# A decoder layer's mixer: the block inverses' transfers move from SyncE's to GpSimd's queue, small GpSimd operations move to VectorE and ScalarE, r, k and v get their own buffer ring, and the ordering model's DMA trips are doubled

## Chip, cores, metric

One core of one Trainium2 chip. The metric is the device time of one launch in microseconds; lower is better.

## What is computed

One step of one hybrid layer for 320 tokens (a prompt of 256 and eight samples of 8), in float32. Cut to what matters here:

```
p = x @ w_in                               # 2048 -> 5408 columns
y_lru  = conv4 -> gated linear recurrence (8 blocks of 128 channels) * gelu(gate)
y_rwkv = RWKV-7: r, k, v with token shift, per token and head (16 heads of 64)
         S = S*w - (S kk) (kk a)^T + v k^T ;  o = S r ; group norm ; gate
x = LN(a*x + [y_lru, y_rwkv] @ w_out)
x = LN(a*x + cross-attention(x, mem))      # mem_k = mem @ wk, mem_v = mem @ wv
x = LN(a*x + relu(x @ w1)^2 @ w2)          # 2048 -> 8192 -> 2048
```

All states (S of prompt and samples, shift rows, convolution rows, recurrence) are outputs too.

## The kernel before

Every weight streams from memory once, in pieces of 128 x 1024 float32 on SyncE's queue (`Stream.load`, L320), three pieces ahead. ScalarE rounds a piece to float32r (`wh<-wraw`), VectorE makes the rest (`wl<-wraw,wh`), and TensorE does three matmuls for each 128 x 128 tile: wh times the high part of the activations, wh times the low part, wl times the high part. These "large matmuls" fill TensorE nearly all the time.

The mixer is the first stage. `linear("w_in", ...)` makes 43 column tiles: three of codes, then for each of eight pairs of heads r, k, v, x, g (48 large matmuls per tile). `linear("wk", ...)` follows with 16 tiles. Beside them run small tasks, written as generators: `rwkv(p)` (L673) for the pair p, `invert(p)` (L885), `sample(p)` (L967) and `lru_task(i)` (L1022).

For the pair p, `rwkv` makes Gram matrices on TensorE (`ps<-AR,BK`), VectorE masks them into the tile GM, and `invert` inverts the triangular blocks of GM: GM goes to memory (bm, two transfers of 64 x 5 x 64, L892), comes back as 40 blocks of 16 x 16 (Mp, L898), GpSimd inverts them in 30 small operations (`tt<-Mp,Xp`, `Xp<-Xp,tt`), Xp goes to memory (bx, L912) and comes back in columns (Xn, two transfers, L917). Then VectorE transposes Xn into XT, and TensorE joins the blocks in four small steps (`ps<-Xn,GM 32x16` is the first, `ps<-XT,Z 32x32` the last). With XT, `rwkv` walks through four chunks, one after the other: R (`ps<-S,AR`, `ps<-UV,GM`), `ps<-R,XT`, copy to UV, `ps<-UV,BT`, new state S. Then come the group norm (`ps<-t,KM`, the spread `ps<-qg,K`) and the gate. The norm's square root and the copies are on ScalarE and VectorE.

All engines work in order, and the order is set when the kernel is built: `Sched` (from L120) keeps a model clock of TensorE and of V, A and G (VectorE, ScalarE, GpSimd). `account` (L136) adds a modelled cost for every operation; `Sched.dma` (L179) puts a task 2.5 us later in the model for a trip to memory; between large matmuls `tick` (L210) puts in the small steps that the model takes to be ready. `drain` (L245) runs tasks without large matmuls between them, until a named task is over: when v of pair i is there, `rwkv(i-3)` must be over (L1099); at x of i, the recurrence i-1 (L1110). The model has no cost for what really happens on the chip; its only effect is the order.

In the order stand on GpSimd's queue, besides the inverses: memset of a column of the scan's tile P (L710), two copies of decays into PT (L777, L778), the memset of `a0` before the recurrence's scan (L1064), a memset and a copy for the convolution (L1108, L1109), and the stores of the states Sp and Ss (L849, L1012), later the stores of mk. On SyncE's queue stand the weights and the inverses' six transfers, and the loads of lora, S0, mem.

Temporaries (`tmp`, L565) come from one ring of 16 buffers; z of r, k, v, which live through most of `rwkv`, come from it as well.

Of the kernel before, what the change touches and what calls it, by code (L numbers as in the profile page):

```python
# [9 lines left out]
F32 = mybir.dt.float32  # L10
# [8 lines left out]
NTOK = 320  # L19
# [85 lines left out]

NTMP = 16
NPB = 3
# [12 lines left out]
class Sched:  # L120
# [15 lines left out]
    def account(self, e, op, a, k):  # L136
# [19 lines left out]
        if e == "V":  # L156
            c = (0.06 + 6.5e-3 * n if op == "reciprocal" else 0.12 + 2.3e-3 * n if op == "tensor_tensor_scan" else
                 0.15 + 1.05e-3 * n)
        elif e == "A":
            c = 0.2 + 0.85e-3 * n  # L160
            f = TABLE.get(a[2]) if op == "activation" else None
            if f is not None:
                if self.table not in f:
                    self.table = f[0]
                    c += 1.3
        else:
            c = 0.15 + 2.1e-3 * n
        t = self.clock if self.cur is None else max(self.clock, self.cur.t)
# [9 lines left out]

    def dma(self, t=2.5):  # L179
        if self.cur is not None:  # L180
            self.cur.t = max(self.clock, self.cur.t) + t
# [163 lines left out]
def body(ctx, tc, I, O):  # L345
# [194 lines left out]
    with ExitStack() as mx_ctx:  # L540
        tp = mx_ctx.enter_context(tc.tile_pool(name="tmp", bufs=NTMP))
        pp = mx_ctx.enter_context(tc.tile_pool(name="pair", bufs=NPB))
        p2 = mx_ctx.enter_context(tc.tile_pool(name="pair2", bufs=2))
# [68 lines left out]
        def blocks(t, h):  # L612

            return bass.AP(tensor=t.tensor, offset=t.offset + 4 * h * MS, ap=[[64, 64], [8 * MS, 5], [1, 64]])
# [4 lines left out]
        def seqs(ap):  # L619
            return ap[:, NP:NTOK].rearrange("p (b t) -> p b t", t=8)  # L620
# [20 lines left out]
        def c5(ap):  # L641
            return ap.rearrange("p (c t) -> p c t", t=64)
# [30 lines left out]
        def rwkv(p, zr, zk, zv):  # L673
# [35 lines left out]
            P = tmp(1 + NTOK)  # L709
            G.memset(P[:, 0:1], 1.0)  # L710
            V.tensor_tensor_scan(P[:, 1:], d0, d1, 0.0, op0=mult, op1=add)
# [64 lines left out]
            PT = pp.tile([128, 12], F32, name="PT")  # L776
            G.tensor_copy(PT[:, 0:4], c5(P1)[:, 0:4, 63])  # L777
            G.tensor_copy(PT[:, 4:12], seqs(P1)[:, :, 7])  # L778
            while sch.alive(("rwkv", p - 2)):
# [68 lines left out]
            yield  # L848
            nc.gpsimd.dma_start(O["Sp"][p], S)  # L849
            o = tmp()  # L850
# [34 lines left out]
        def invert(p, GM, res):  # L885
# [5 lines left out]
            for h in range(2):  # L891
                nc.sync.dma_start(blocks(bm[b], h), GM[HS[1 - h], h, :, 0, :])  # L892
            sch.dma()
# [3 lines left out]
            yield  # L897
            nc.sync.dma_start(Mp, diag(bm[b]))  # L898
            Mp = Mp.rearrange("p c r -> p r c")
# [4 lines left out]
            for j in range(15):  # L904
# [5 lines left out]
                if j % 5 == 4:  # L910
                    yield
            nc.sync.dma_start(diag(bx[b]), Xp)  # L912
            sch.dma()
            yield
            Xn = p1.tile([128, 5, 64], F32, name="Xn")
            for h in range(2):
                nc.sync.dma_start(Xn[HS[1 - h]], blocks(bx[b], h))  # L917
            sch.dma()
# [48 lines left out]
        def sample(p, S0, AR, XT, GM, B4, UV, PT, res):  # L967
# [43 lines left out]
            tt(S0, S0, PT[:, 4:12].unsqueeze(2).to_broadcast([128, 8, 64]), mult)  # L1011
            nc.gpsimd.dma_start(O["Ss"][p], S0)  # L1012

# [8 lines left out]
        def lru_task(i, ue):  # L1022
# [40 lines left out]
            tt(r0, r0, t8, add)  # L1063
            G.memset(a0, 0.0)  # L1064
            yield
# [19 lines left out]
        def on_win(m, ps):  # L1085
# [8 lines left out]
            elif kind in "rkv":  # L1094
                t = tmp()
                shifted({"r": 0, "k": 8, "v": 16}[kind] + i, ps, t)
# [6 lines left out]
            elif kind == "x":  # L1103
# [3 lines left out]
                A.copy(us[:, :, 3:11], ps[:, NP:NTOK].rearrange("p (b t) -> p b t", t=8))  # L1107
                G.memset(ue[:, 0:3], 0.0)  # L1108
                G.tensor_copy(us[:, :, 0:3], vec("cv", 24 * i, 24).rearrange("p (b t) -> p b t", t=3))  # L1109
                sch.drain(("lru", i - 1))  # L1110
# [620 lines left out]
```

## Time and profile before

| | us |
|---|---|
| median of 3 runs (lowest, highest) | 2060.48 (2059.3, 2062.53) |
| the profiled execution | 2060.96 |
| its span | 2059.2 |
| TensorE busy (96% of the span) | 1986.5 |
| VectorE, ScalarE, GpSimd busy | 1049.3, 890.4, 407.6 |
| mean granted TensorE clock, of full speed | 0.981 |

The page gives the busy time of each engine and then forty slices of the span; the mixer with its w_in and wk is slices 1 to 12 (0 to about 600 us). Times in the trace are from the start of the span. "Idle before <- X" is the idle time of an engine ahead of an instruction and what ended it. An operation's line is nearly always L284, the helper that records it, so instructions are told apart by their tiles: out<-in.

### The profile page before, as it was taken

To read this page: it belongs to the slowest core of one execution; us is meant where nothing else is said; L and a number is where in the kernel's file an instruction comes from. 1 tells how busy PE (TensorE), PEld (TensorE's weight loads), DVE (VectorE), ACT (ScalarE), POOL (GpSimd) and SP (SyncE) were. 2 spreads that over 40 slices of the span, in tenths; PEclk is the share of its full clock that TensorE was granted. 3 is DMA by queue.
4 is the path that set the end of the run, shared out by engine and by line. 5 is a ranking of instruction groups with operands and counts; after the bars stand their busy time and mean duration, and the time that the engine had idled before them with its cause. 6 is when DMAs were issued, how large, how long until landed. Compare 5 with 4: busy or idle time off the path is not lost.

```text
span 2059.2 us, 38107 instructions
## 1 busy us (share of the span) xinstructions
PE 1986.5 (96%) x15750; PEld 1889.1 (92%) x15750; DVE 1049.3 (51%) x1608; ACT 890.4 (43%) x1459; POOL 407.6 (20%) x677
## 2 busy tenths in 40 slices
PE   7989989998999999999999999999999999999996
PEld 7987878887898999988899999999999999999996
DVE  5566566666555445544466544443444444443444
ACT  5555455554535434643434633334323333233333
POOL 0121222220411244422143500001000000001133
PEclk9999999998999999999999999999999999999998
DMA  6443343333557764688744444444444444444442
GB/s 236 149 120 93 94 116 117 111 118 126 168 170 238 251 224 156 208 322 298 268 138 139 140 149 152 151 147 153 148 150 153 144 154 151 147 153 149 149 147 89
DMA packets 120846, 333.80 MB, mean 162 GB/s; under 512 B 33072, under 2 KB 42576, under 8 KB 120672
## 3 DMA queue, kind: packets, MB, share of 16 engines
q1 hardware_dynamic: 105536, 279.59, 42.8%
q0 software_dynamic: 15136, 51.77, 7.1%
q8 instruction: 123, 2.02, 0.4%
q14 instruction: 51, 0.42, 0.1%
HBM read 315.66 MB, written 15.65 MB: 161 GB/s over the span
## 4 chain that ended last, share of the span: by engine, by line
PE 85%; POOL 5%; DMA 4%; DVE 3%; issue 1%; ACT 1%; SPq 0%; POOLq 0%; ACTq 0%; DVEq 0%
PE ps L284 85%; POOL Xp L284 2%; POOL tt L284 2%; DMA Mp<-bm 1%; DMA bm<-GM 1%; DVE wl L284 1%; DMA t<-in_x 1%; DMA Xn<-bx 0%; DVE t L284 0%; DMA wraw<-in_w_in 0%; POOL u L284 0%; DMA t<-in_mem 0%; ACT u L284 0%; DVE GM L284 0%; DVE u L284 0%
## 5 line engine op out<-in xcount | busy, mean ns | idle before, releaser
L284 DVE TENSOR_TENSOR wl<-wraw,wh 128x1024 fp32r<-128x1024 f32 x494 | 611.5, 1241 | 580.6 <-ACT wh L284 579.9
L284 ACT CAST wh<-wraw 128x1024 fp32r<-128x1024 f32 x502 | 525.7, 1049 | 632.5 <-PE ps L284 576.8
L284 PE MATMUL ps<-u,wh 128*128 128x320 f32 (+1 forms) x3424 | 771.3, 315 | 12.4 <-ACT u L284 11.5
L284 PE MATMUL ps<-r,wh 128*128 128x320 f32 x3072 | 680.8, 310 | 3.0 <-ACT r L284 1.8
L284 PEld LDWEIGHTS ps<-u,wh 128*128 128x128 f32 x3424 | 577.1, 193 | 32.0 <-ACT u L284 12.2
L284 PE MATMUL ps<-u,wl 128*128 128x320 f32 (+1 forms) x1712 | 529.7, 309 | 0.0
L284 PEld LDWEIGHTS ps<-r,wh 128*128 128x128 f32 x3072 | 514.6, 188 | 7.9 <-issue 3.8
L284 PE MATMUL ps<-r,wl 128*128 128x320 f32 x1536 | 475.5, 310 | 0.0
L284 PEld LDWEIGHTS ps<-u,wl 128*128 128x128 f32 x1712 | 329.6, 193 | 0.0
L284 PEld LDWEIGHTS ps<-r,wl 128*128 128x128 f32 x1536 | 289.1, 188 | 0.0
L284 PE MATMUL ps<-h,wh 128*128 128x320 f32 x1024 | 225.6, 309 | 0.0
L284 POOL TENSOR_TENSOR r<-r 128x320 f32<-128x320 f32 x64 | 46.0, 720 | 722.6 <-ACT r L284 722.6
L284 PEld LDWEIGHTS ps<-h,wh 128*128 128x128 f32 x1024 | 171.4, 188 | 0.2
L284 PE MATMUL ps<-h,wl 128*128 128x320 f32 x512 | 158.2, 309 | 0.0
L284 DVE TENSOR_TENSOR u<-u,ps 128x320 f32<-128x320 f32 x134 | 61.7, 484 | 80.8 <-PE ps L284 77.8
L284 ACT ACTIVATE r<-ps 128x320 f32<-128x320 f32 x64 | 28.0, 437 | 157.7 <-PE ps L284 157.7
L284 PEld LDWEIGHTS ps<-h,wl 128*128 128x128 f32 x512 | 96.1, 188 | 0.0
L284 POOL TENSOR_TENSOR s<-s,u 128x320 f32<-128x320 f32 x42 | 65.8, 1568 | 91.6 <-DVE u L284 91.4
L284 POOL TENSOR_TENSOR tt<-Mp,Xp 40x15 f32<-40x15 f32 (+7 forms) x120 | 47.7, 397 | 181.7 <-DMA Mp<-bm 173.2
L284 PE MATMUL ps<-wh,u 128*128 128x512 f32 x256 | 79.9, 390 | 0.0
L284 ACT ACT_TABLE_LOAD x47 | 60.3, 1283 | 9.2 <-DVE mxs L284 7.6
L284 PEld LDWEIGHTS ps<-wh,u 128*128 128x128 f32 x256 | 48.1, 188 | 10.1
(239 smaller groups left out, 1553.1 us busy)
## 6 DMA issues: line engine op xcount, KB each, us to landing
wraw<-in_w SPq DMA_DIRECT2D x256, 512.0 KB
wraw<-in_w_in SPq DMA_DIRECT2D x86, 512.0 KB
wraw<-in_wk SPq DMA_DIRECT2D x32, 512.0 KB
wraw<-in_wv SPq DMA_DIRECT2D x32, 512.0 KB
wraw<-in_w_out SPq DMA_DIRECT2D x32, 512.0 KB
kv<-in_cache_k POOLq DMA_DIRECT2D x32, 512.0 KB, 6.7
wraw<-in_wq SPq DMA_DIRECT2D x32, 512.0 KB
kv<-in_cache_v POOLq DMA_DIRECT2D x32, 512.0 KB, 9.0
```

The costliest lines, as they stand in the source:

```text
L284: r = f(*a, **k)
```

## The change

1. The six transfers of each `invert` are issued on GpSimd's queue.
2. The stores of Sp and Ss are issued on SyncE's queue.
3. Three small memsets for each pair or block move from GpSimd to VectorE, three copies from GpSimd to ScalarE. On GpSimd's queue there are then only the inverses until the stores of mk.
4. z of r, k, v get a ring of six buffers; the ring of the other temporaries goes from 16 to 10.
5. In the ordering model a trip to memory takes 5.0 us instead of 2.5, and a GpSimd operation 0.22 us plus its elements instead of 0.15.

```diff
--- before.py
+++ after.py
@@ -103,7 +103,7 @@
 NDER = _n
 
 
-NTMP = 16
+NTMP = 10
 NPB = 3
 MARGIN = 0.3
 TURN = 0.093
@@ -164,7 +164,7 @@
                     self.table = f[0]
                     c += 1.3
         else:
-            c = 0.15 + 2.1e-3 * n
+            c = 0.22 + 2.1e-3 * n
         t = self.clock if self.cur is None else max(self.clock, self.cur.t)
         end = max(self.free[e], t) + c
         self.free[e] = end
@@ -176,7 +176,7 @@
         t = self.clock if self.cur is None else max(self.clock, self.cur.t)
         return min(costs, key=lambda e: max(self.free[e], t) + costs[e][0] + costs[e][1] * n)
 
-    def dma(self, t=2.5):
+    def dma(self, t=5.0):
         if self.cur is not None:
             self.cur.t = max(self.clock, self.cur.t) + t
 
@@ -539,6 +539,7 @@
     mv = drp.tile([128, 2, D], F32, name="mv")
     with ExitStack() as mx_ctx:
         tp = mx_ctx.enter_context(tc.tile_pool(name="tmp", bufs=NTMP))
+        zp = mx_ctx.enter_context(tc.tile_pool(name="z", bufs=6))
         pp = mx_ctx.enter_context(tc.tile_pool(name="pair", bufs=NPB))
         p2 = mx_ctx.enter_context(tc.tile_pool(name="pair2", bufs=2))
         p1 = mx_ctx.enter_context(tc.tile_pool(name="one", bufs=1))
@@ -707,7 +708,7 @@
             V.scalar_tensor_tensor(rk, zr, vec("rk", p), X2[:, 0], op0=mult, op1=mult)
 
             P = tmp(1 + NTOK)
-            G.memset(P[:, 0:1], 1.0)
+            V.memset(P[:, 0:1], 1.0)
             V.tensor_tensor_scan(P[:, 1:], d0, d1, 0.0, op0=mult, op1=add)
             P0, P1 = P[:, :NTOK], P[:, 1:]
             V.reciprocal(qn, qn)
@@ -774,8 +775,8 @@
                 copy(UV4[h, i], p4[i][h, 192:256])
             free(4)
             PT = pp.tile([128, 12], F32, name="PT")
-            G.tensor_copy(PT[:, 0:4], c5(P1)[:, 0:4, 63])
-            G.tensor_copy(PT[:, 4:12], seqs(P1)[:, :, 7])
+            A.copy(PT[:, 0:4], c5(P1)[:, 0:4, 63])
+            A.copy(PT[:, 4:12], seqs(P1)[:, :, 7])
             while sch.alive(("rwkv", p - 2)):
                 yield 1.0
 
@@ -846,7 +847,7 @@
                 if c < 3:
                     yield PE_HH
             yield
-            nc.gpsimd.dma_start(O["Sp"][p], S)
+            nc.sync.dma_start(O["Sp"][p], S)
             o = tmp()
             A.copy(o[:, :NP], po[:, :NP])
             free()
@@ -889,13 +890,13 @@
             b = p % 2
             yield
             for h in range(2):
-                nc.sync.dma_start(blocks(bm[b], h), GM[HS[1 - h], h, :, 0, :])
+                nc.gpsimd.dma_start(blocks(bm[b], h), GM[HS[1 - h], h, :, 0, :])
             sch.dma()
             Mp = p1.tile([40, 16, 16], F32, name="Mp")
             Xp = p1.tile([40, 16, 16], F32, name="Xp")
             tt = p1.tile([40, 64], F32, name="tt")
             yield
-            nc.sync.dma_start(Mp, diag(bm[b]))
+            nc.gpsimd.dma_start(Mp, diag(bm[b]))
             Mp = Mp.rearrange("p c r -> p r c")
             sch.dma()
             nc.gpsimd.memset(Xp, 0.0)
@@ -909,12 +910,12 @@
                 G.tensor_tensor(Xp[:, j + 1:, 0:w], Xp[:, j + 1:, 0:w], o, op=add)
                 if j % 5 == 4:
                     yield
-            nc.sync.dma_start(diag(bx[b]), Xp)
+            nc.gpsimd.dma_start(diag(bx[b]), Xp)
             sch.dma()
             yield
             Xn = p1.tile([128, 5, 64], F32, name="Xn")
             for h in range(2):
-                nc.sync.dma_start(Xn[HS[1 - h]], blocks(bx[b], h))
+                nc.gpsimd.dma_start(Xn[HS[1 - h]], blocks(bx[b], h))
             sch.dma()
             XT = p2.tile([128, 5, 64], F32, name="XT")
             yield
@@ -1009,7 +1010,7 @@
             free()
             yield
             tt(S0, S0, PT[:, 4:12].unsqueeze(2).to_broadcast([128, 8, 64]), mult)
-            nc.gpsimd.dma_start(O["Ss"][p], S0)
+            nc.sync.dma_start(O["Ss"][p], S0)
 
 
         lru = {}
@@ -1061,7 +1062,7 @@
             t8 = p1.tile([128, 8], F32, name="t8")
             tt(t8, a0, vec("h0", 8 * i, 8), mult)
             tt(r0, r0, t8, add)
-            G.memset(a0, 0.0)
+            V.memset(a0, 0.0)
             yield
             h = ta
             V.tensor_tensor_scan(h, a, r, 0.0, op0=mult, op1=add)
@@ -1092,7 +1093,7 @@
             if kind == "c":
                 sch.run(codes(i, ps), "codes")
             elif kind in "rkv":
-                t = tmp()
+                t = zp.tile([128, NTOK], F32, name="z")
                 shifted({"r": 0, "k": 8, "v": 16}[kind] + i, ps, t)
                 z[kind, i] = t
                 if kind == "v":
@@ -1105,8 +1106,8 @@
                 us = ue[:, 259:347].rearrange("p (b t) -> p b t", t=11)
                 A.copy(ue[:, 3:259], ps[:, :NP])
                 A.copy(us[:, :, 3:11], ps[:, NP:NTOK].rearrange("p (b t) -> p b t", t=8))
-                G.memset(ue[:, 0:3], 0.0)
-                G.tensor_copy(us[:, :, 0:3], vec("cv", 24 * i, 24).rearrange("p (b t) -> p b t", t=3))
+                V.memset(ue[:, 0:3], 0.0)
+                A.copy(us[:, :, 0:3], vec("cv", 24 * i, 24).rearrange("p (b t) -> p b t", t=3))
                 sch.drain(("lru", i - 1))
                 sch.add(lru_task(i, ue), ("lru", i), 1.0)
             else:
```

What it makes of the order. On GpSimd, around the end of the first inverse, before:

```order
L284 TENSOR_TENSOR tt<-Mp,Xp 40x60
L284 TENSOR_TENSOR Xp<-Xp,tt 40x6x10
L284 MEMSET t 128x8
L284 TENSOR_TENSOR tt<-Mp,Xp 40x55
L284 TENSOR_TENSOR Xp<-Xp,tt 40x5x11
L284 TENSOR_TENSOR tt<-Mp,Xp 40x48
L284 TENSOR_TENSOR Xp<-Xp,tt 40x4x12
L284 TENSOR_TENSOR tt<-Mp,Xp 40x39
L284 TENSOR_TENSOR Xp<-Xp,tt 40x3x13
```

and with the change:

```order
L284 TENSOR_TENSOR tt<-Mp,Xp 40x28
L284 TENSOR_TENSOR Xp<-Xp,tt 40x2x14
L284 TENSOR_TENSOR tt<-Mp,Xp 40x15
L284 TENSOR_TENSOR Xp<-Xp,tt 40x15
L913 DMA bx_129<-Xp 40x16x16
L918 DMA Xn<-bx_129 64x5x64 x2
L893 DMA bm_128<-GM 64x5x64 x2
L899 DMA Mp<-bm_128 40x16x16
L902 MEMSET Xp 40x256
L903 MEMSET Xp 40x16
```

The memset 128x8 is `a0` of the recurrence (L1064); it stood behind the first twenty of the inverse's thirty operations, and in later inverses behind ten to thirty of them (in the third it stands ahead). With the change nothing but the inverse stands there, its transfers follow its last operation, and the next inverse's first three follow these.

On SyncE, around the second inverse, before:

```order
L320 DMA wraw<-in_w_in 128x1024
L892 DMA bm_125<-GM 64x5x64 x2
L320 DMA wraw<-in_w_in 128x1024 x2
L898 DMA Mp<-bm_125 40x16x16
L802 DMA lg<-in_lora 128x256
L804 DMA S_1778<-in_S 128x512
L320 DMA wraw<-in_w_in 128x1024 x2
L912 DMA bx_127<-Xp 40x16x16
L320 DMA wraw<-in_w_in 128x1024
L917 DMA Xn<-bx_127 64x5x64 x2
L320 DMA wraw<-in_w_in 128x1024 x2
```

and with the change:

```order
L805 DMA S_1707<-in_S 128x512
L320 DMA wraw<-in_w_in 128x1024 x5
L1013 DMA out_Ss<-S_1129 128x512
L1021 DMA lruw<-in_lru_w 128x256
L320 DMA wraw<-in_w_in 128x1024 x2
L654 DMA lw<-in_lora 128x128
L320 DMA wraw<-in_w_in 128x1024 x4
L850 DMA out_Sp<-S 128x64
L320 DMA wraw<-in_w_in 128x1024
L1013 DMA out_Ss<-S_1707 128x512
```

The weights (`wraw`) no longer stand behind bm, Mp, bx and Xn; stores of Ss and Sp stand between them instead.

On TensorE, at the point where v of pair 3 is there and `rwkv(0)` is drained (after 1008 large matmuls in both), the small steps without a large matmul between them were, before:

```order
L284 MATMUL ps<-t,KM 32x80 x4
L284 MATMUL ps<-GM,UV_1458 64x64 x2
L284 MATMUL ps<-um_2564,B_1457 64x512
L284 MATMUL ps<-um_2565,B_1457 64x512
L284 MATMUL ps<-R,XT 64x64 x2
L284 MATMUL ps<-AR,S 64x64 x2
L284 MATMUL ps<-UV,BT 64x64 x2
L284 MATMUL ps<-GM,UV 64x64 x2
L284 MATMUL ps<-qg,K 128x80 x4
L284 MATMUL ps<-sg,lg 128x320 x2
L284 MATMUL ps<-S,AR 64x64 x2
L284 MATMUL ps<-UV,GM 64x64 x2
```

and are with the change (the first 12 of 30 rows):

```order
L284 MATMUL ps<-R,XT 64x64 x2
L284 MATMUL ps<-AR,S 64x64 x2
L284 MATMUL ps<-Xn,GM 32x32 x10
L284 MATMUL ps<-UV,BT 64x64 x2
L284 MATMUL ps<-GM,UV 64x64 x2
L284 MATMUL ps<-XT,Z 32x32 x10
L284 MATMUL ps<-t,KM 128x320
L284 MATMUL ps<-UV,GM 64x64 x2
L284 MATMUL ps<-AR,S_1707 64x16 x16
L284 MATMUL ps<-R,XT 64x64 x2
L284 MATMUL ps<-UV,BT 64x64 x2
L284 MATMUL ps<-GM,UV 64x64 x2
```

Steps of pair 1's inverse and chunks (`ps<-Xn,GM`, `ps<-XT,Z` and those behind) have come into this run; a second one, of 28 rows, stands after 1728 large matmuls, where before small and large ones alternated. The inverse's steps move back: between a pair's Gram matrices and its first `ps<-Xn,GM 32x16` there stand, for the pairs 0 to 7, 141, 120, 102, 117, 129, 126, 117, 153 large matmuls before, and 240, 237, 111, 195, 207, 123, 219, 228 with the change (the two runs lie in the stretches of the pairs 2 and 5). The last small step of the mixer stands after 2694 large matmuls before and after 2742 with the change; wk ends at 2832 in both. Behind that TensorE's order is the same.

## Rows read from the trace of the kernel before

**Rows 1.** Busy time of TensorE over the span (the page's first part).

```profile
PE 1986.5 (96%) x15750; PEld 1889.1 (92%) x15750; DVE 1049.3 (51%) x1608; ACT 890.4 (43%) x1459; POOL 407.6 (20%) x677
```

**Rows 2.** Waits of PE from 0 to 560 us: total, times, longest.

```profile
PE ps L284 <- DMA Xn<-bx: 12.3, 4, 5.6
...
PE ps L284 <- DVE UV L284: 8.5, 3, 4.9
PE ps L284 <- DVE S L284: 5.8, 2, 4.7
PE ps L284 <- DVE R L284: 3.4, 1, 3.4
PE ps L284 <- DVE um L284: 3.0, 1, 3.0
```

**Rows 3.** Chain of waits, 86 to 116 us: start, length, what.

```profile
88.25 3.42 DMA bm<-GM
91.73 3.60 DMA Mp<-bm
...
109.60 2.58 DMA bx<-Xp
...
112.85 2.56 DMA Xn<-bx
```

**Rows 4.** Timeline of POOL, then DVE, at 158 us: start, length, what [idle before <- releaser].

```profile
157.83 0.11 POOL L284 MEMSET t<- 128x8 f32 x1
```

```profile
157.97 0.82 DVE L284 TENSOR_TENSOR_SCAN t<-t 128x320 f32<-128x320 f32 x1 [5.96 <-POOL t L284]
```

**Rows 5.** Waits of DVE, then ACT, from 0 to 560 us.

```profile
DVE t L284 <- POOL t L284: 31.2, 7, 6.5
```

```profile
ACT u L284 <- DMA t<-in_mem: 11.6, 3, 6.7
```

**Rows 6.** Stretches behind waits: us, busy by engine, granted clock PEclk, DMA share, GB/s.

```profile
115.50:121.00 5.50, 5.46 (x59) 5.45 (x60) 5.32 (x10) 1.54 (x4) 0.68 (x4) 0.52 0.08 13
...
411.80:418.00 6.20, 6.18 (x126) 5.76 (x127) 4.66 (x11) 5.14 (x13) 0.00 (x0) 1.00 0.45 151
...
473.50:479.20 5.70, 5.68 (x19) 4.50 (x19) 2.69 (x4) 3.45 (x6) 0.95 (x4) 0.50 0.57 177
...
541.10:550.80 9.70, 9.67 (x91) 9.18 (x92) 4.12 (x8) 6.24 (x13) 1.07 (x2) 0.50 0.74 240
```

**Rows 7.** Timeline of PE: large matmuls at 208 us, then at 229 us.

```profile
207.88 0.45 PE L284 MATMUL ps<-u,wh 128*128 128x320 f32 x2
...
208.31 0.46 PE L284 MATMUL ps<-u,wh 128*128 128x320 f32 x2
```

```profile
229.34 0.73 PE L284 MATMUL ps<-u,wh 128*128 128x320 f32 x2
...
230.14 0.73 PE L284 MATMUL ps<-u,wh 128*128 128x320 f32 x2
```

**Rows 8.** DMA issues on POOL's queue: count, KB each, median us from issue to landing.

```profile
mk<-t POOLq DMA_DIRECT2D x16, 128.0 KB, 2.8
...
out_Sp<-S POOLq DMA_DIRECT2D x8, 32.0 KB, 1.8
...
bx<-d POOLq DMA_DIRECT2D x2, 22.5 KB, 6.1
```

**Rows 9.** Groups of POOL: count, busy us, mean ns of one, idle before.

```profile
L1333 POOL DMA_DIRECT2D kv<-mk x4 | 3.0, 761 | 9.0 <-PE ps L284 9.0
...
L284 POOL MEMSET t<- 128x8 f32 x8 | 0.9, 111 | 23.2 <-DVE t L284 23.2
```

**Rows 10.** Timeline of PE in the drained run of pair 0.

```profile
214.46 0.34 PE L284 MATMUL ps<-UV,BT 128*64 128x64 f32 x4 [0.56 <-DVE UV L284]
...
215.62 1.12 PE L284 MATMUL ps<-qg,K 128*128 128x80 f32 x8 [0.70 <-DVE qg L284]
```

**Rows 11.** Tile Mp: duration of POOL's products, ns min/median/max.

```profile
L284 POOL TENSOR_TENSOR tt<-Mp,Xp x120: 202/275/2462, 95.5 to 537.6; 40x15 f32<-40x15 f32 x16, 40x28 f32<-40x28 f32 x16, 40x39 f32<-40x39 f32 x16, 40x48 f32<-40x48 f32 x16
```

## The prediction

> **What bounds it now.** TensorE is busy for 96% of the span [rows 1], so only what keeps it idle or slow can be gained. I read its waits first, for the mixer alone, then what each had waited for, then the clock behind them. In the mixer TensorE waits 12.3 us for Xn, the inverse that comes back from memory, in four pieces, and 20.7 us for VectorE: tiles UV, S, R and um [rows 2]. Why VectorE is late stands in two rows of one moment [rows 4]: the recurrence's scan waited 5.96 us for a memset of eight columns, which lasts 0.11 us but stood on GpSimd's queue behind twenty operations of an inverse. VectorE waits so 31.2 us in seven pieces [rows 5]. Four of TensorE's waits end with the operation right behind such a scan: um 3.0, R 3.4 and two of the three for UV, 8.5 [rows 2] less the 0.56 of [rows 10]; together 14.3 us.
>
> After a wait the clock falls. Nine of the waits, the longer ones, are each followed by a stretch at 1.2 GHz, of 3.4 to 9.7 us; the first and the last of these and one of the middle are in [rows 6], granted at 0.50 to 0.52. Behind the shortest of the four waits for Xn, before 411.8, it stayed at 1.00 [rows 6]. At full speed three large matmuls take 0.43 us (208.31 - 207.88), at half speed 0.80 (230.14 - 229.34) [rows 7], so a microsecond at half speed loses (0.80 - 0.43)/0.80 = 0.46.
>
> **What goes.**
> - Xn: 12.3 us of waits; behind three of the four stand 5.3, 6.4 and 3.4 us at half speed, 15.1 x 0.46 = 6.9. Together 19.2. They go because TensorE's order puts the first step on Xn later, not because Xn comes sooner. From GM on its way to Xn landed the first inverse took 27.2 us (88.25 to 112.85 + 2.56) [rows 3], 14.3 of it GpSimd's operations (95.33 to 109.60). TensorE had 141 large matmuls for it, and waited 5.6 [rows 2]. Now it has 240: 99 x 0.143 = 14.2 us more, 8.6 more than was missing. The pairs 1, 3, 4, 6 and 7 get 75 to 117 more, 11 to 17 us. Only the pairs 2 and 5 get no more large ones (+9, -3), but a drained run stands in their stretch.
> - GpSimd's small operations: 14.3 us of waits, and behind them 5.6, 6.1, 3.4 and 9.7 us at half speed, 24.8 x 0.46 = 11.4. Together 25.7. Nothing of VectorE waits for GpSimd any more.
> - The load of mem: ScalarE waits 11.6 us for it in three pieces [rows 5]; TensorE's longest wait for S, 4.7 us [rows 2], with 5.7 us at half speed behind it [rows 6], 2.6, comes of one of them, 7.3 in all. Its transfer was issued late because VectorE had stood still for the memset and SyncE behind it; ScalarE still stops for the landing. I take half, 3.6.
>
> Gone: 19.2 + 25.7 + 3.6 = 48.5.
>
> **What is added.**
> - The six transfers on GpSimd. No row shows these there. The nearest are mk, 2.8 us from issue to landing, Sp 1.8, and 6.1 for the small bx fill at the start [rows 8]; one issue costs GpSimd up to 0.76 us [rows 9]. With mk's, the nearest in kind (SBUF to memory, amid the running weights): 4 trips x 2.8 + 2 second issues x 0.76 + 14.3 = 27.0 us, the same as before; with bx's 40.2. So the inverse is not faster. For the pairs 2, 5 and, for the mk stores that still stand between on its queue, 7, I put 1 us of wait each: 3. The lower end is 0, the upper is a rival below.
> - Two drained runs. After 1008 large matmuls 30 rows of small steps follow each other instead of 12, after 1728 there are 28 instead of none. The work itself moves and costs nothing; the gaps between dependent steps, which large matmuls filled, are new. The run of before shows two gaps, 0.56 and 0.70 [rows 10], over three dependent steps: 0.42 each. Each new run holds a chain of seven steps, and a second chain of three or four of the older pair beside it. If the second hides in the first: 14 x 0.42 - 1.3 (the run of before) = 4.6 us. If nothing hides, at 0.70 for each of 21 steps, and each run is followed by the middle stretch at half speed, 6.4 x 0.46: 14.7 + 5.9 - 1.3 = 19.3. I take the middle, 12, since neither chain is clearly apart.
> - Six operations a pair on VectorE and ScalarE, 48 in all, at 0.11 us for a memset [rows 9] and some more for a copy: both engines are busy about half of the time [rows 1], and most of these stand where the next operation waits anyway. Nothing; without that cover 48 x 0.2 = 10 us spread over two engines, of which TensorE would see little.
> - Stores of Sp and Ss on SyncE ahead of weights: they wait for a VectorE operation which stands ahead of the low part that frees the next piece's buffer, so the next weight waits as long in any case. Nothing. In return weights no longer stand behind Mp's and Xn's round trips.
> - The rings. r, k, v get two pairs' room; the rest has ten for 14 allocations a pair, where all had 16 for 17. A writer now waits for readers of ten allocations ago. All of these were put in order ahead of it; nothing, unless an engine lags by some twenty microseconds.
> - The mixer's last small step moves 48 large matmuls back but stays 90 ahead of wk's end, so nothing sticks out there.
>
> Sum: 2060.96 (the profiled execution) - 48.5 + 12 + 3 = 2027.5. The median of the runs is 0.5 lower, so **2027 us**. Its own range is 2014 to 2045, from the ends of the drained runs and of the mem term, and some of the GpSimd term left.
>
> **Rivals.**
> - *Slow trips (slower).* If a trip on GpSimd's queue takes 6.1 us as bx's fill did [rows 8], an inverse takes 40.2, 13 more than before. By the large matmuls above, six pairs have some 11 us of room and two some 4: 6 x 2 + 2 x 9 = 30 us of waits, and eight stretches of 6.4 us at half speed, 23. 2027 - 3 + 53 = 2077. It decides from about 5.6 us a trip. For it: the transfers are of 64 and 256 bytes a piece. Against it: bx's fill was one of four issued at once, at the start, beside the first weights; Sp and mk later landed in 1.8 and 2.8. Chance 0.09.
> - *Issues held up by VectorE.* GpSimd's products last 0.275 us in the median but up to 2.46 [rows 11]: something holds GpSimd for up to 2.2 us. If it holds half of an inverse's six issues so, 6.6 us more, only the pairs 2 and 5 are late, by 2.6 each, and each with 2.9 for the clock: 2027 + 11 = 2038. The Trainium skill, page "SBUF — State Buffer", section "Who interferes with whom", speaks against this change: VectorE in a two-port mode locks GpSimd out of a shared port pair, and GpSimd cannot write descriptors for its DMAs meanwhile. The same section says that a two-input VectorE operation contends only with GpSimd's reads, and most of VectorE's work here is of that kind, which would hold the products and not the issues. The one row of issues, four of kv at a mean of 0.76 us [rows 9], shows no such hold. Chance 0.05.
> - *The waits come back.* In-order engines find another last wait: the ring of ten, ScalarE's new copies behind a scan, or the mem landings. If VectorE or ScalarE stops as long as VectorE did for GpSimd, the 25.7 us return: 2053. For it: VectorE waits for ScalarE at many places now. Against it: these others rarely reach TensorE today. Chance 0.13; in a sixth of it the whole gain is eaten.
> - *All of it.* The drained runs cost 4.6, the mem wait goes wholly, no Xn wait is left: 2060.5 - 52.2 + 4.6 = 2013, and some us below it if short waits of other kinds go as well. Chance 0.10.
> - *Nothing moves*: the model's order merely changes the places of the waits and the time stays within 0.2%. Chance 0.06, which leaves 0.57 for the forecast.
>
> **The numbers.** Two runs of this kernel differ by up to 3 us, so 0.2%, 4 us, is about what a measurement can tell. Faster by more than that: forecast 0.57, all of it 0.10, issues held up 0.05, and most of the waits that come back, 0.11: 0.83. Same: 0.06 and the rest of these, 0.08. Slower: 0.09. The range reaches from 2006, a little below the case of all, to 2060, which takes in the waits that come back; outside are the slow trips, most of the unchanged case and the extremes, under 0.2.
>
> **What would show it.** Right: no wait of VectorE for GpSimd in the mixer; no or one short wait of TensorE for Xn; an inverse of 26 to 30 us; two places, after 1008 and 1728 large matmuls, with gaps of a few us in all, perhaps each with a half-speed stretch; the clock at 1.00 in most mixer slices; everything behind wk as before, only earlier. Wrong: landings over 5 us on GpSimd's queue and TensorE waiting for Xn in most pairs; or the same sum of waits on TensorE with ScalarE's or VectorE's temporaries as what ended them; or drained runs of over 20 us each.

## The result, and the profile after

| | before | after |
|---|---|---|
| median, us (4 runs of each, taken together) | 2059.89 | 2036.45 |
| lowest, highest | 2054.26, 2062.53 | 2034.55, 2038.85 |
| the profiled execution, its span | 2060.96, 2059.2 | 2038.85, 2036.8 |
| mean granted clock, of full speed | 0.981 | 0.985 |

The ratio of the times is 0.989, with a 95% interval of 0.9866 to 0.9915: faster by 1.1%. Forecast were 2027 us, from 2006 to 2060.

TensorE is busy for 8.1 us less than in [rows 1], and it waits less. Less of its work runs at half speed, 40.9 us in the mixer against 54.4, which at 0.46 makes 6.2 of the 8.1. The waits of PE from 0 to 560 us after the change (total, times, longest):

```profile
PE ps L284 <- ACT u L284: 13.3, 3, 6.7
PE ps L284 <- DVE R L284: 9.7, 4, 4.7
PE ps L284 <- ACT R L284: 4.2, 1, 4.2
PE ps L284 <- DVE UV L284: 2.0, 2, 1.3
```

Against [rows 2] the four waits for Xn are gone, and the waits for um and of UV shrank from 11.5 to 2.0 us. VectorE's row `t <- POOL t` [rows 5] has no successor: VectorE waits nowhere in the mixer for a GpSimd operation. But the waits for R have grown from 3.4 to 13.9 us (9.7 by VectorE, 4.2 by ScalarE). Two places hold most of them. The first is the mem stretch, 440 to 490 us. Timelines of PE, VectorE, ScalarE and SyncE's queue there:

```profile
448.23 0.48 PE L284 MATMUL ps<-R,XT 64*64 64x64 f32 x4 [4.71 <-DVE R L284]
```

```profile
445.91 1.46 DVE L284 TENSOR_TENSOR u<-t,u 128x256 fp32r<-128x256 f32 x3 [5.75 <-ACT u L284]
```

```profile
445.48 1.44 ACT L284 CAST u<-t 128x256 fp32r<-128x256 f32 x3 [7.19 <-DMA t<-in_mem]
...
454.48 1.37 ACT L284 CAST u<-t 128x256 fp32r<-128x256 f32 x4 [3.95 <-DMA t<-in_mem]
...
462.14 1.41 ACT L284 CAST u<-t 128x256 fp32r<-128x256 f32 x4 [4.30 <-DMA t<-in_mem]
```

```profile
429.12 10.83 SPq L320 DMA_DIRECT2D wraw<-in_wk  x3
440.19 1.02 SPq L1013 DMA_DIRECT2D out_Ss<-S  x1
441.26 1.97 SPq L1122 DMA_DIRECT2D t<-in_mem  x4
...
450.69 1.81 SPq L1122 DMA_DIRECT2D t<-in_mem  x4
```

Mem's sixteen tiles come in four groups of four. The first three are issued only when ScalarE already stands for them, so ScalarE, in order, waits for the whole trip: 7.19, 3.95, 4.30 us. In the first, 3.0 of the 7.19 us are the queue: ScalarE stands from 438.29 us, and the loads follow three weights and a store at 441.26. VectorE stands behind ScalarE (5.75 us), the small copy R behind VectorE, TensorE behind R. ScalarE's row for in_mem is now 17.9 us in 5 pieces; it was 11.6 [rows 5].

The second place is the last pair's XT, in timelines of POOL, DVE and PE:

```profile
523.79 0.90 POOL L913 DMA_DIRECT2D bx<-Xp  x1 [0.59 <-issue]
528.82 1.37 POOL L918 DMA_DIRECT2D Xn<-bx  x2 [4.12 <-PE ps L284]
```

```profile
532.92 0.51 DVE L284 STREAM_TRANSPOSE XT<-Xn 128x320 f32<-128x320 f32 x1 [6.46 <-DMA Xn<-bx]
```

```profile
533.60 0.48 PE L284 MATMUL ps<-R,XT 64*64 64x64 f32 x4 [3.62 <-DVE R L284]
```

The transfer into Xn is issued when bx, issued 5.0 us earlier, has landed. The row puts its wait down to TensorE, but TensorE's last step on the Xn of the pair before lies 35 us back, and in the version with mem's tiles loaded ahead (below) the same row names bx. PE of this kernel, then POOL of that version:

```profile
493.42 0.50 PE L284 MATMUL ps<-Xn,GM 32*32 32x32 f32 x20
```

```profile
515.38 1.38 POOL L918 DMA_DIRECT2D Xn<-bx  x2 [4.77 <-DMA bx<-Xp]
```

VectorE stands 6.46 us at XT, and TensorE 3.62 us for the R behind it. Stretches of the changed kernel (us, busy by engine as in [rows 6], PEclk, DMA share, GB/s):

```profile
195.50:209.20 13.70, 11.49 (x114) 7.83 (x114) 5.52 (x18) 6.42 (x13) 5.28 (x14) 0.50 0.10 16
369.00:380.00 11.00, 9.27 (x121) 6.63 (x118) 9.79 (x28) 5.95 (x18) 9.12 (x25) 1.00 0.33 120
...
465.50:472.00 6.50, 5.63 (x29) 5.12 (x29) 5.42 (x10) 5.04 (x14) 0.00 (x0) 0.50 0.26 84
...
533.50:540.00 6.50, 6.40 (x114) 5.91 (x114) 1.75 (x5) 1.85 (x4) 1.07 (x2) 0.50 0.32 101
```

The first is the drained run after 1008 large matmuls: half speed for its whole length. The second, after 1728, stays at full speed. The other two stand behind waits, in the mem stretch and behind the last XT.

### The profile page after: what moved, and what is told of

It reads as the page before. It is cut to its first block, busy times and chain, and to the rows that moved or that the text cites. A ratio compares the mean times of both kernels' runs of the same rounds, so it can differ in the third digit from the quotient of the medians.

```text
span 2036.8 us, 38079 instructions
## 1 busy us (share of the span) xinstructions
PE 1978.4 (97%) x15750; PEld 1883.3 (92%) x15750; DVE 1056.1 (52%) x1654; ACT 894.4 (44%) x1464; POOL 434.1 (21%) x661
## 2 busy tenths in 40 slices
DMA packets 103149, 333.82 MB, mean 164 GB/s; under 512 B 13808, under 2 KB 23824, under 8 KB 102976
## 4 chain that ended last, share of the span: by engine, by line
PE 93%; DMA 2%; DVE 2%; ACT 1%; issue 1%; POOL 1%; SPq 0%; POOLq 0%; ACTq 0%; DVEq 0%
PE ps L284 93%; DMA t<-in_mem 1%; DMA wraw<-in_w_in 1%; POOL u L284 0%; DVE u L284 0%; DVE wl L284 0%; DMA t<-in_x 0%; ACT u L284 0%; ACT wh L284 0%; DVE t L284 0%; POOL r L284 0%; DMA Xn<-bx 0%; DVE S L284 0%; ACT L284 0%; POOL wl L284 0%
## 5 line engine op out<-in xcount | busy, mean ns | idle before, releaser
L284 DVE TENSOR_TENSOR wl<-wraw,wh 128x1024 fp32r<-128x1024 f32 x494 | 612.5, 1243 | 569.3 <-ACT wh L284 568.8
L284 PE MATMUL ps<-u,wh 128*128 128x320 f32 (+1 forms) x3424 | 761.6, 313 | 14.1 <-ACT u L284 13.3
L284 PEld LDWEIGHTS ps<-u,wh 128*128 128x128 f32 x3424 | 571.6, 191 | 31.2 <-ACT u L284 13.8
L893 POOL DMA_DIRECT2D bm<-GM x16 | 10.9, 685 | 241.2 <-DVE GM L284 241.2
```

Source lines behind the costliest of these rows:

```text
L284: r = f(*a, **k)
L893: nc.gpsimd.dma_start(blocks(bm[b], h), GM[HS[1 - h], h, :, 0, :])
```

## The experiments

The theory at the outset: of the change's five parts the trips in the model take the Xn waits away and the moved small operations the memset's waits, each by itself; the mem stretch lost what was missing against the forecast. Each kernel was timed beside runs of the kernel before on the same chip, so ratios to that are compared. In a ratio 0.001 is 2 us. Diffs are against the kernel named.

### The memset alone

```diff
 (the kernel before, lru_task)
-            G.memset(a0, 0.0)
+            V.memset(a0, 0.0)
```

> The kernel before, with one edit: the lru's memset of a0 is issued by VectorE and not by GpSimd. Theory (the memset behind the inverse's products is what made VectorE and then TensorE wait; the prediction put 25.7 us on it and its like): VectorE no longer waits for POOL at the scan, the waits of PE for um and the two for UV behind it go, and the time falls by 14 to 26 us, to 2034 to 2047; the Xn waits (12.3 us) stay. Rival (the memset's waits only move to the next late operation): under 6 us, 2054 to 2061.

Measured: 2075.31 us, ratio 1.0081 (1.0058 to 1.0103). Neither: it is slower. VectorE no longer waits for POOL anywhere, yet its waits for XT doubled, from 26.2 us to those of the first row. The second row is that of the kernel before. The timelines of DVE and PE at pair 2 show how:

```profile
DVE XT L284 <- DMA Xn<-bx: 53.0, 7, 10.4
```

```profile
DVE XT L284 <- DMA Xn<-bx: 26.2, 7, 6.0
```

```profile
214.39 0.28 DVE L284 SCALAR_TENSOR_TENSOR S<-ps,PT,ts 128x64 f32<-128x64 f32 x1 [0.27 <-PE ps L284]
224.70 0.51 DVE L284 STREAM_TRANSPOSE XT<-Xn 128x320 f32<-128x320 f32 x1 [10.02 <-DMA Xn<-bx]
...
225.71 0.21 DVE L284 COPY R<-ps 128x64 f32<-128x64 f32 x1
```

```profile
225.97 0.48 PE L284 MATMUL ps<-R,XT 64*64 64x64 f32 x4 [7.00 <-DVE R L284]
```

Freed of the memset, VectorE is at the transpose of Xn ten microseconds before Xn lands, and all that the order has put behind the transpose waits with it, the older pair's R among it. The memset's waits had been time that VectorE would have lost at XT: it waits 26.8 us more there, for 31.2 less behind the memset [rows 5]. So the two terms of the forecast are one: with the inverse too early in the order, VectorE waits at the one place or the other. The edit is not the move alone, though: the model books the memset on another engine, and the order shifts with it. Between a pair's Gram matrices and its first step on Xn there now stand 135, 117, 114, 123, 123, 123, 126, 147 large matmuls, between 6 fewer and 12 more than before. What the shift costs by itself is not shown.

### The trips alone

```diff
 (the kernel before, Sched)
-    def dma(self, t=2.5):
+    def dma(self, t=5.0):
```

> The kernel before, with one edit: a trip to memory counts 5.0 us and not 2.5 in the order's model. Theory (the two waits are two causes: the longer trips take the Xn waits of PE away, 19.2 us with their half speed, and cost about 10 for the first drained run; the memset of a0 behind the inverse's products still holds VectorE and through it um and UV): VectorE's waits for POOL t stay near 31 us, and 2045 to 2054. Rival (one cause: with Xn later in TensorE's order VectorE has slack and the memset's waits no longer reach TensorE): waits of VectorE for POOL remain, but none of PE for um or UV over 2 us, and 2032 to 2041. Second rival (the drained runs give it all back): 2056 or more.

Measured: 2017.12 us, ratio 0.9799 (0.9781 to 0.9817), faster than the rival and than the whole change. Ahead of a pair's first step on Xn there stand 48 to 93 more large matmuls than in the kernel before, for pair 2 only 6 more. In the order a trip of 5.0 also moves GpSimd's products back, and `a0`'s memset stands behind five pairs of products where, for pair 1, it stood behind ten. The timelines of POOL and DVE at pair 1:

```profile
145.52 0.12 POOL L284 MEMSET t<- 128x8 f32 x1 [0.98 <-DVE t L284]
```

```profile
146.68 0.91 DVE L284 TENSOR_TENSOR_SCAN t<-t 128x320 f32<-128x320 f32 x1
```

GpSimd is early and waits 0.98 us for VectorE, where VectorE had waited 5.96 for it [rows 4]. VectorE's waits for POOL t are 0.2 us in all. So even the rival was half wrong: the memset's waits do not merely stop to reach TensorE, they are gone. The span fell by 45.2 us. The prediction's two terms, 19.2 for Xn and 25.7 for GpSimd's operations, make 44.9: one number of the model's was enough for both. That the sums agree so closely is in part chance: the trace also has 6 us less in the mem stretch and about 8 more in the drained run (waits of 2.9 us and 13.7 at half speed, less the 1.3 of before), which the two terms do not hold.

The rest of the change therefore costs some 19 us; the next runs look for it.

### The changed kernel without one of its parts

```diff
 (the changed kernel, invert: all six transfers)
-            nc.gpsimd.dma_start(Mp, diag(bm[b]))
+            nc.sync.dma_start(Mp, diag(bm[b]))
...
```

> The changed kernel with the six kinds of transfers of the inverse issued by SyncE again; the order of TensorE's work is the changed one. Theory (the longer trips in the model moved TensorE's first step on Xn back, and that, not the queue that issues, is why its Xn waits are gone): no Xn wait over 1 us on PE, and 2034 to 2044, the same as the changed kernel within 4 us; the mem loads then stand behind the inverse's waits on SyncE's queue as before, which may cost up to 7 of it. Rival (the queue is what did it): Xn waits of 8 us or more come back and it takes 2048 or more.

Measured: 2033.85 us, 0.9881 (0.986 to 0.9903): the same as the changed kernel, and no Xn wait on PE. The order does it, not the queue.

```diff
 (the changed kernel, rwkv and sample)
-            nc.sync.dma_start(O["Sp"][p], S)
+            nc.gpsimd.dma_start(O["Sp"][p], S)
...
-            nc.sync.dma_start(O["Ss"][p], S0)
+            nc.gpsimd.dma_start(O["Ss"][p], S0)
```

> The changed kernel with the two stores of states (Sp and Ss) issued by GpSimd again; nothing else, and TensorE's order is the same. Theory (the store of Ss stands on SyncE's queue ahead of mem loads and waits up to 10.5 us there for VectorE, so that the mem loads of the stretch 440 to 480 us are late): the wait of PE at 448 us (4.71 us and 3.4 us of half speed behind it) shrinks or goes, and the time falls by 3 to 8 us, to 2029 to 2034. Rival (a mem load is late because it is issued only when its tile comes free, store or no store): within 2 us of the changed kernel. Second rival (on GpSimd the waiting store holds up the last inverse): slower by 3 us or more, with the wait for XT or Xn at 530 us longer.

Measured: 2038.49 us, 0.9902 (0.988 to 0.9925): the same. SyncE's queue and PE in the mem stretch:

```profile
426.51 10.85 SPq L320 DMA_DIRECT2D wraw<-in_wk  x3
437.41 2.62 SPq L1122 DMA_DIRECT2D t<-in_mem  x4
```

```profile
445.30 0.48 PE L284 MATMUL ps<-R,XT 64*64 64x64 f32 x4 [4.37 <-DVE R L284]
```

With the store away the loads stand behind weights that wait just as long (10.85 us for three, 10.83 with the store). The wait for R stays, 4.37 us. The theory of the store is out.

```diff
 (the changed kernel)
-NTMP = 10
+NTMP = 16
...
-                t = zp.tile([128, NTOK], F32, name="z")
+                t = tmp()
```

> The changed kernel with r, k, v in the one ring of 16 tiles again, and nothing else undone; TensorE's order is the same. Theory (the ring of their own leaves the rest 10 tiles and not 16; mem's tiles come from those 10, so that their loads wait for an older tile, and that is the common cost of the changed kernel, of it with the transfers on SyncE and of it with the small operations back, against the kernel before with longer trips alone, 2017.1): the loads of mem go out earlier, PE's waits at 448 and 466 us fall below 1.5 each, and it takes 2016 to 2025. Rival (the ring holds nothing; what costs is each time something else, the queue in one and the small operations in the other): 2032 to 2039.

Measured: 2037.17 us, 0.9879 (0.9858 to 0.9901): the same, with mem's loads where they were. The theory of the ring is out, too, and the converse says the same:

> The kernel before with two edits: trips of 5.0 and the ring of their own for r, k, v (10 and 6 tiles for 16). Theory (the ring is what costs): 10 to 20 us slower than the trips alone, 2027 to 2037, with the mem loads issued one group at a time and PE's waits of 3 us or more at 445 to 485 us back. Rival (the ring costs nothing): within 3 us of the trips alone, 2014 to 2020.

Measured for the trips with the ring of their own (the edit above, reversed): 2016.46 us, 0.9771 (0.9751 to 0.9792), like the trips alone.

```diff
 (the changed kernel: all six small operations)
-            V.memset(a0, 0.0)
+            G.memset(a0, 0.0)
...
-            A.copy(PT[:, 0:4], c5(P1)[:, 0:4, 63])
+            G.tensor_copy(PT[:, 0:4], c5(P1)[:, 0:4, 63])
...
```

> The changed kernel with the small operations (the memsets of P, a0 and ue, the copies into PT and us) on GpSimd again; TensorE's order then is that of the kernel before with only the longer trips, so that against that kernel it differs by the queue that issues the inverse's transfers and by the ring. Theory (with small operations on GpSimd a queue that also waits for the inverse's transfers holds them longer, so that VectorE's wait for POOL grows past 31 us and reaches TensorE): 2048 to 2062. Rival (the queue and the small operations make no difference once the trips are long): 2033 to 2042.

Measured: 2032.59 us, 0.9872 (0.9853 to 0.9891), just below the rival's range: with long trips no difference by the small operations can be told; VectorE's waits for POOL t are 0.2 us. One sentence of the expectation was wrong: TensorE's order here is not that of the trips alone, since the 0.22 of a GpSimd operation in the model moves it. PE's waits lie in the mem stretch again, and the last pair's Xn has one:

```profile
448.53 0.34 PE L284 MATMUL ps<-UV,BT 128*64 128x64 f32 x4 [4.54 <-DVE UV L284]
...
457.45 0.48 PE L284 MATMUL ps<-S,AR 64*64 64x64 f32 x4 [4.26 <-DVE S L284]
...
538.03 0.73 PE L284 MATMUL ps<-Xn,GM 16*32 16x16 f32 x40 [2.81 <-DMA Xn<-bx]
```

### The model's cost of a GpSimd operation

```diff
 (the kernel before with trips of 5.0, Sched)
-            c = 0.15 + 2.1e-3 * n
+            c = 0.22 + 2.1e-3 * n
```

> The kernel before with two edits: trips of 5.0, and 0.22 us and not 0.15 as the fixed cost of a GpSimd operation in the order's model. Every kernel of this study with 0.22 took 2021 to 2038, and those with the longer trips and 0.15 took 2010 to 2017. TensorE's order is here the one of the changed kernel with the small operations back on GpSimd (2032.6), from which it differs by the queue of the inverse's transfers, the queue of the two stores and the ring. Theory (the 0.22 moves the order of all engines in a way that costs the waits at 445 to 480 us again): 2027 to 2034, with waits of PE over 2 us in that stretch. Rival (the order is as good; the transfers on GpSimd and the stores on SyncE cost it): 2014 to 2020, with no such wait but the one for u at 466 us.

Measured: 2024.16 us, 0.9841 (0.9823 to 0.9859): above the rival and below the theory. The 0.22 alone costs about 0.0042, some 9 us; its interval lies clear of that of the trips alone. The place is the one expected, in the timelines of ACT and PE:

```profile
448.77 1.40 ACT L284 CAST u<-t 128x256 fp32r<-128x256 f32 x4 [7.75 <-DMA t<-in_mem]
```

```profile
451.04 0.48 PE L284 MATMUL ps<-S,AR 64*64 64x64 f32 x4 [6.40 <-DVE S L284]
```

With 0.15 the second and third group of mem are issued together (442.67, eight loads) and ScalarE stops once for both; with 0.22 the first and second go together, the third stands behind two weights and ScalarE stops 7.75 us for it. From here to the small operations back is 0.0031 more, about 6 us, the transfers on GpSimd, the stores on SyncE and the ring, with intervals that overlap a little. Which of them is not shown: none of the three undone alone gained anything that can be told in the changed kernel. The traces point to the queue. The wait for the last pair's Xn above, 2.81 us with 6.8 at half speed behind it (5.9 in all), is missing here, where the transfers are on SyncE's queue; and in the changed kernel with the transfers on SyncE TensorE waits 2.61 us for the R behind the last XT, not 3.62.

### Mem's tiles ahead

```diff
 (the changed kernel; on_win behind the last pair's rwkv task, and mem_prod)
+                    if i == 7:
+                        for j in range(4):
+                            mem_load(j)
...
+        def mem_load(kt):
+            if kt < KT and kt not in mems:
+                mems[kt] = t = tmp(NP)
+                nc.sync.dma_start(t, I["mem"][kt // 4][:, kt % 4, :])
...
-            t = tmp(NP)
-            nc.sync.dma_start(t, I["mem"][kt // 4][:, kt % 4, :])
-            Mm.put(kt, t)
+            mem_load(kt)
+            Mm.put(kt, mems[kt])
+            mem_load(kt + 2)
```

> The changed kernel with mem's tiles loaded ahead: four loads are issued once the last pair's rwkv task is added, and each later one two tiles ahead of its use. Theory (the waits of PE at 448, 456, 466 and 483 us, 13.2 us, and the half speed behind them, 17 us at 0.46, are the lateness of the mem loads): ACT's wait for in_mem (17.9 us) falls below 6, and the time falls by 8 to 18 us, to 2019 to 2029. Rival (the same tiles of the pool are then missing for the tasks, and the waits move to them): 2032 to 2042, with new waits of PE for R, S or UV in 430 to 490 us.

Measured: 2024.59 us, 0.9838 (0.9815 to 0.9861): 0.0052 below the changed kernel, some 11 us, as the theory has it. ScalarE still waits 8.0 us for in_mem, more than expected. The waits at 448 and 483 us shrank to 0.9 and 1.5, the one for R by ScalarE stayed, 3.53.

On top of it, the loads on GpSimd's queue (`nc.gpsimd.dma_start` in `mem_load`), and, apart from that, the stores of mem_k on SyncE's (`nc.sync.dma_start` for mk and out_mem_k):

> The version with mem's tiles loaded ahead, with those loads issued by GpSimd, which stands idle between 440 and 475 us (36.6 us for a mk store), and not by SyncE, where they stand behind weights that wait; TensorE's order is the same. Theory (what is left of ACT's wait for in_mem, 8.0 us, and of PE's waits for u and R at 456 and 470 us, 5 us and 6.8 of half speed, is the queue in front of the loads): in_mem waits under 3 us, and 3 to 8 us faster than with SyncE, 2016 to 2022. Rival (the loads wait for a free tile, or the transfer itself is what is waited for): within 2 us of it. Second rival (a load that waits on GpSimd for its tile holds the last pairs' inverses): slower, with Xn or XT waits in 430 to 530 us.

> The version with mem's tiles loaded ahead, with the stores of mem_k (mk and out_mem_k, four or more pairs of 1.15 us between the last pair's products and ahead of its bx) issued by SyncE; TensorE's order is the same. Theory (the wait of PE for R at 519 us, 3.4 us and 6.8 us of half speed behind it, is the last pair's Xn, which is late by the stores on GpSimd's queue, 3.4 us): VectorE's wait for XT there falls from 6.2 to under 3.5, the wait for R to under 0.5, and the time by 4 to 7 us, to 2017 to 2021. Rival (on SyncE the stores stand ahead of weights of wk, and TensorE waits for u or wh there): slower by 2 us or more. Second rival (VectorE's products set the inverse's pace): within 2 us.

Measured: 2022.1 us, 0.9821 (0.9797 to 0.9845), and 2021.71 us, 0.9819 (0.98 to 0.9838). Both are 0.0017 to 0.0019 below their base, inside the intervals: no gain can be told. The first mechanism moved as named: with GpSimd's queue ScalarE's row for in_mem is the first below. The second did so in part: with mem_k's stores on SyncE the last pair's XT waits 4.28 us and R 1.44 (second and third), where its base had 6.24 and 3.40 and under 3.5 and 0.5 were expected. XT itself starts at 518.6 us in both; VectorE came to it 2 us later.

```profile
ACT u L284 <- DMA t<-in_mem: 0.8, 3, 0.3
```

```profile
518.66 0.51 DVE L284 STREAM_TRANSPOSE XT<-Xn 128x320 f32<-128x320 f32 x1 [4.28 <-DMA Xn<-bx]
```

```profile
519.34 0.33 PE L284 MATMUL ps<-R,XT 64*64 64x64 f32 x4 [1.44 <-DVE R L284]
```

The same loads ahead, in the kernel before with trips of 5.0:

> The kernel before with trips of 5.0, the one ring of 16, and mem's tiles loaded ahead (four at the last pair's rwkv task, then two ahead of use). Theory (what in_mem still makes ACT wait, 11.9 us, and PE for R and u at 450 and 466 us, 3.7 us and 3.4 of half speed, is the late issue): 3 to 7 us faster than the trips alone, 2010 to 2014. Rival (the transfers issued earlier take tiles that the tasks want): 2016 or more.

Measured: 2010.65 us, 0.9748 (0.9731 to 0.9766), the fastest of all: 2.5% below the kernel before, 1.4% below the changed one. PE's waits from 0 to 560 us:

```profile
PE ps L284 <- ACT u L284: 10.4, 3, 7.0
PE ps L284 <- DVE RO L284: 1.7, 1, 1.7
PE ps L284 <- DVE S L284: 1.2, 3, 0.8
```

Of the 10.4 us, 9.4 are the start of the program (7.0 for the first input and 2.4 at 27 us). Little is left to wait for in the mixer.

### One account for all runs

For the profiled execution of each run: all waits of PE from 0 to 560 us, the stretches there at half speed, and waits + 0.46 x half speed as the loss.

| kernel | waits | half speed | loss | loss less that of before | span less that of before |
|---|---|---|---|---|---|
| before | 47.3 | 54.4 | 72.3 | | |
| memset alone | 62.7 | 71.4 | 95.5 | +23.2 | +15.8 |
| changed kernel | 34.6 | 40.9 | 53.4 | -18.9 | -22.4 |
| ring undone | 34.6 | 34.0 | 50.2 | -22.1 | -27.5 |
| stores on GpSimd | 34.4 | 30.6 | 48.5 | -23.8 | -26.6 |
| transfers on SyncE | 31.6 | 34.1 | 47.3 | -25.0 | -28.6 |
| small operations back | 28.5 | 34.0 | 44.1 | -28.2 | -27.5 |
| mem ahead | 24.9 | 23.8 | 35.8 | -36.5 | -37.9 |
| mem ahead, mem_k's stores on SyncE | 24.2 | 23.9 | 35.2 | -37.1 | -39.3 |
| mem ahead on GpSimd | 21.8 | 23.9 | 32.8 | -39.5 | -40.2 |
| trips and 0.22 | 22.7 | 20.4 | 32.1 | -40.2 | -40.5 |
| trips alone | 18.7 | 17.1 | 26.6 | -45.7 | -45.2 |
| trips and ring | 19.9 | 13.6 | 26.2 | -46.1 | -43.9 |
| trips and mem ahead | 16.1 | 13.6 | 22.4 | -49.9 | -51.4 |

But for the memset alone and the ring undone (7.4 and 5.4 us off), the loss gives each of these spans within 4 us: most of what a kernel gains or loses lies in the mixer's waits and in the clock behind them.

## Why the prediction was right, and where its steps were wrong

The sum was for the profiled execution: 2060.96 - 48.5 + 15 = 2027.5; it took 2038.85. The time came 11.4 us late and still lay in the range, since errors of both signs were added: the direction and the reason for Xn were right, that the total was not further off was luck.

- **Xn, 19.2 us gone:** right, by the mechanism named. No wait of PE for Xn is left, with the transfers on either queue, so it is TensorE's order. Of the three waits of 1 us, those for pairs 2 and 5 did not come; the one for pair 7 came through VectorE and was larger (below).
- **The inverse is not faster:** right, and it is slower than the 27.0 us estimated. The first one goes from bm's issue at 89.52 us to the issue of Xn's second half, 119.1, and with the median landing of 3.4 ends near 122: 32 to 33 us. For all but the last pair the order has room for that.
- **GpSimd's small operations, 25.7 us gone:** the waits went as foretold, but the step has the wrong cause. The memset moved alone costs 0.8%; the longer trips take its waits away with the memset left where it was. "Together 25.7" was right as a size only because the trips came with it. At the end of the mixer, where R had waited 3.4 us behind the last memset, it now waits 3.62 us behind the last XT, with 6.8 us at half speed 6.7 in all: the last pair's inverse is late, for which the sum had 1 us.
- **The drained runs, 12:** measured 10.1. The first has gaps of 3.4 us and 13.7 us at half speed (6.3), the second gaps of 1.7, and 1.3 of the run before goes off. The estimate had taken the gaps larger and the half-speed stretch shorter.
- **The load of mem, 3.6 gone:** this step failed. The forecast saw the load late because VectorE had stood still for the memset, and took half of 7.3 us as gone. In the changed kernel the waits at 448, 456, 466 and 483 us (13.2 us) with 17.0 us at half speed (7.8) make 21.0; in the kernel before, S 4.7 and u 2.0 with 10.2 us at half speed made 11.4. So 9.6 were added where 3.6 were to go: 13 us, more than the whole error. What was missed is that a load issued at its use costs its trip even with little ahead of it (3.95 and 4.30 us). In both kernels the groups are issued one at a time, but in the changed order ScalarE came to more of them too early: it waits in five pieces, not three. Loading ahead won 0.0052 in the changed kernel and 0.0051 with the trips alone.
- **Stores on SyncE, rings, small operations on the new engines: nothing.** Right for each within the intervals. The reading of the new trace that put the wait at 448 us on the store of Ss was wrong.
- **Not in the sum:** the cost of a GpSimd operation in the model. The forecast named it nowhere. It costs 9 us by the run that has it alone beside the trips, by the trace in the mem stretch, so that these are not to be added to the 13 above. In the changed kernel it was not undone.
- **Rivals.** "Slow trips" had the trips partly right: median landings of 2.5 to 4.1 us, not the 6.1 from which it was worked out, and the order had room for them but at the last pair. "The waits come back" is what happened in part, with the mem landings it named. "Issues held up by VectorE" did not happen. The sixteen issues of Xn on POOL (duration ns min/median/max, first and last start) show no hold:

```profile
L918 POOL DMA_DIRECT2D Xn<-bx x16: 672/698/712, 117.7 to 529.5; - x16
```

The Trainium skill, page "SBUF — State Buffer", section "Who interferes with whom", would have GpSimd's descriptors wait while VectorE runs in a two-port mode. The trace shows no such wait in these issues, with VectorE busy for half of the time. Most of that is `wl`, with two inputs (612.5 of 1056.1 us), for which the prediction itself expected no hold on the issues, so the hold is not ruled out.

What stays open: which of transfers, stores and ring costs the 6 us between the trips with 0.22 and the small operations back; what 0.15 would give in the changed kernel; and whether other values of either constant do better, since each was run at two values alone and every edit that touches the model shifts the whole order.

## What to carry to other kernels

Where a table of model costs sets the order of in-order engines, a wait and its cure are properties of the order. Before an operation is moved off a queue on which someone waits, ask where the waiting engine will stand next: here the freed VectorE only arrived earlier at a transfer that had not landed. A load that is issued where it is used costs its trip on the engine that uses it; issue it ahead before tuning anything around it, and test each part of a change alone, since the best part may be hidden by the others. Such a test is not clean where the edit also enters the model: read the new order beside the time.

## What was not expected of the hardware

- An issue on GpSimd's queue costs time on GpSimd by the number of pieces. From the groups of POOL in the changed kernel (count, busy us, mean ns of one, idle before), 0 to 560 us:

```profile
L893 POOL DMA_DIRECT2D bm<-GM x16 | 10.9, 685 | 241.2 <-DVE GM L284 241.2
L899 POOL DMA_DIRECT2D Mp<-bm x8 | 7.3, 914 | 22.9 <-DMA bm<-GM 22.9
...
L1133 POOL DMA_DIRECT2D out_mem_k<-t x9 | 4.9, 547 | 0.0
```

A store of 128 rows takes 547 ns, GM's 64 x 5 rows 685, Mp's 40 x 16 rows 914, while the bytes fall (128, 80 and 40 KB).

- By the view of the issues, bm and Xn land no later by GpSimd's queue than by SyncE's. In the changed kernel (DMA issues: count, KB each, median us to landing) bm lands after 2.5 and Xn after 3.4 us:

```profile
bm<-GM POOLq DMA_DIRECT2D x16, 80.0 KB, 2.5
Xn<-bx POOLq DMA_DIRECT2D x16, 80.0 KB, 3.4
...
Mp<-bm POOLq DMA_DIRECT2D x8, 40.0 KB, 4.1
bx<-Xp POOLq DMA_DIRECT2D x8, 40.0 KB, 3.7
```

```profile
bm<-GM SPq DMA_DIRECT2D x16, 80.0 KB, 3.4
Xn<-bx SPq DMA_DIRECT2D x16, 80.0 KB, 3.7
```

The second piece is the same view of the changed kernel with the transfers on SyncE: 3.4 and 3.7. For Mp and bx that view has no landing. On SyncE's queue the kernel before shows 3.60 and 2.58 for them in one inverse [rows 3], against medians of 4.1 and 3.7 here, so for these no gain is shown.
- The transfers on GpSimd's queue leave fewer small packets: 13808 under 512 bytes in the changed kernel, 34096 with them on SyncE, for the same bytes.
